# A hybrid attention and recurrence trunk: one input projection of the recurrence moved from the sliding-window branch to the first differential-attention head

## The chip, the cores and the metric

The kernel runs on one core of one Trainium2 chip. The metric is the device time of one execution in microseconds (us). Engines are called PE (TensorE), DVE (VectorE), ACT (ScalarE), POOL (GpSimd) and SP (SyncE, which here only issues DMAs); PEld is PE's loading of weights. Most executions of a kernel agree within 0.3%.

## The reference, cut to what matters

Two layers run over 128 context tokens and 1024 latent tokens of width 1024. Each layer normalises and modulates its input to `h`, projects `h` by one wide matrix, feeds three branches, gates each branch with its own SiLU path, and merges them:

```python
(q_a, k_a, v_a, g_a, x_b, g_b, q_c, k_c, v_c, g_c, merge), gate = mixer_front(x, mod, P['norm_g'], P['w_in'])
oa = attn_a_latent(q_a, k_a, v_a, ck_a, cv_a, P['sink_a'])       # windowed attention, 8 heads
xb = centred_conv(x_b, P['conv_w'], P['conv_b'])
ob, _ = rglru_bidir(xb, st, P)                                    # gated linear recurrence, 512 channels
oc = diff_attn(q_c, k_all, v_all, lam, P['subln_c'], lam_init)    # differential attention, 4 heads
return mixer_tail(x, gate, oa, g_a, ob, g_b, oc, g_c, merge, P)
```

Everything is float32. The change concerns only when `x_b` and `g_b` are computed.

## The kernel before, in words

All 1152 tokens are held as nine tiles of 128. `h` stays in SBUF for the whole layer as a high and a low part; every float32 product is made of three matmuls (high by high, high by low, low by high) in `mm3`. A weight block of 1024 x 128 columns is loaded by one DMA into `wsraw`, cast on ACT into `wsh`, and its remainder is taken on POOL in four pieces into `wsl` (`ws_load`); the three buffers come from a ring W of seven. The block then meets the nine token tiles in three chunks of 384 columns (`ws_chunk`, 8 x 3 = 24 matmuls, one PSUM buffer `ps_s` of four). The projection to queries, keys and values works the other way round, one token tile at a time (`tok_gemm`, weights `uwh`, `uwl`), also 24 matmuls of 384 columns.

`unit_phase` is the stage around the change. In its foreground run the four heads of branch C, and then the four head pairs of branch A. Each walks over five groups of token tiles, `GR` = (0), (1,2), (3,4), (5,6), (7,8): queries are transposed (`q_conv`), scores are made (`c_probs` or `a_probs`: matmuls, row maximum on DVE, exponential on ACT), and one group later the probabilities are transposed and multiplied with the values (`c_pv` or `a_pv`, called through `flush`). At the end of a head or pair `c_finish` or `a_finish` multiplies with the SiLU gate.

Beside the foreground runs the generator `background`, which yields once after each chunk of 24 matmuls. It projects the next head's queries, keys and values (nine chunks), the current head's gate (`gate_silu`, three chunks), then the remaining queries of branch A (`a_gemm2`, nine chunks), the gates of its four pairs (three each), and the recurrence's two inputs for each of four channel tiles (`lru_x(L, ct)`, three chunks of `x_b` and three of `g_b`, stored to DRAM as `xsp` and `gsp` for the tail). `step(n)` takes `n` chunks of it. The tables say how many are taken where: `BG0` in the first C head (before its context keys, then after each group), `BGQ` in the other heads, `BGA` in branch A. Foreground calls go through `fg`, which gives their instructions a priority 2000 places ahead. The Tile framework settles the order of instructions on each engine when the kernel is built, and the engine then takes its queue in that order.

Before the change the first C head has 6+2+2+1+1+0 = 12 steps, the others 12. Branch A has 3 steps, then 2 after each of twenty groups, 43 of the 45 there are; the last two follow behind the last pair. `lru_x(L, 0)` to `lru_x(L, 3)` come behind the gates of pairs 1, 2, 3 and 3. After `unit_phase` comes the tail, which computes the recurrence from the stored tiles beside the merge projections.

Of the kernel before, what the change touches and what calls it, by code (L numbers as in the profile page):

```python
# [37 lines left out]
XPOS = 1  # L38

BGQ = (2, 2, 2, 3, 2, 1)  # L40
BG0 = (6, 2, 2, 1, 1, 0)
BGA = (3, 2, 2, 2, 2, 2)

RINGS = {"S": 26, "P": 7, "T": 2, "Q": 2, "W": 7, "D": 3, "E": 2, "cx": 1, "tab": 1}

# [9 lines left out]
def hybrid_dit_kernel(ctx, tc, I, O):  # L55
# [14 lines left out]
    def al(tag, name, *shape):  # L70

        return big.tile([128] + list(shape), F32, tag=tag, name=name, bufs=RINGS[tag])
# [13 lines left out]
    def dma(out, in_):  # L86
        nc.sync.dma_start(out=out, in_=in_)
# [13 lines left out]
    def stt(out, a, s, b, op0, op1):  # L101
        V.scalar_tensor_tensor(out=out, in0=a, scalar=s, in1=b, op0=op0, op1=op1)  # L102
# [46 lines left out]
    def split(hi, lo, raw, eh="A", el="P"):  # L149

        if eh == "A":
            acopy(r(hi), raw)
        else:
            V.tensor_copy(r(hi), raw)
        if el == "P":
            psub(r(lo), raw, hi)
        else:
            tt(V, r(lo), raw, hi, ALU.subtract)

    def ws_load(wcols, kt):  # L160

        raw = al("W", "wsraw", kt, 128)
        wcols(raw)
        hi, lo = al("W", "wsh", kt, 128), al("W", "wsl", kt, 128)
        split(hi, lo, raw)
        return hi, lo

    def w_in_cols(l, c0):
        def f(lo):
            dma(lo, I["w_in"][l, :, c0:c0 + 128].rearrange("(k p) n -> p k n", p=128))  # L170
        return f
# [19 lines left out]
    def ws_chunk(L, hi, lo, c):  # L191
        p = ps("s", 384)
        for k in range(KT):
            a, b = hchunk(L, c, k)
            mm3(p, hi[:, k, :], lo[:, k, :], a, b, k == 0, k == KT - 1)
        return p
# [153 lines left out]
    def load_wu(L, groups, early=False):  # L350

        src = I["w_in"][L.l].rearrange("(k p) n -> p k n", p=128)
        raws, w = [], []

        def conv(raw):
            m = raw.shape[1]
            hi, lo = al("W", "uwh", m, 384), al("W", "uwl", m, 384)
            split(hi, lo, raw, "A", "P")
            return [(hi[:, j, :], lo[:, j, :]) for j in range(m)]
        for k0 in (0, 3, 6):  # L360
            m = min(3, KT - k0)
            raw = al("W", "wuraw", m, 384)
            for g, c0 in enumerate(groups):
                dma(raw[:, :, 128 * g:128 * g + 128], src[:, k0:k0 + m, c0:c0 + 128])
            raws.append(raw)
            if not early:
                w += conv(raws.pop())
        for raw in raws:
            w += conv(raw)
        return w  # L370
# [72 lines left out]
    def gate_silu(L, c0, put):  # L443

        gate = al("S", "gate", NTOK)

        def f(c, p):
            t = al("D", "gt", 384)
            A.activation(out=t, in_=p, func=AF.Tanh, scale=0.5)
            stt(gate[:, c * 384:(c + 1) * 384], t, 1.0, p, ALU.add, ALU.mult)  # L450
        hi, lo = ws_load(w_in_cols(L.l, c0), KT)
        put(gate)
        for c in range(3):
            f(c, ws_chunk(L, hi, lo, c))
            yield
# [5 lines left out]
    def c_groups(h):  # L461
        return [CQC + 128 * h, CKC + 128 * h, CVC + 128 * h]
# [264 lines left out]
    def unit_phase(L):  # L727

        l = L.l
        a_groups = [CQA, CKA, CVA]  # L730
        pend = None

        done = None

        def flush():
            nonlocal pend, done
            d, done = done, None
            if pend:
                pend()
                pend = None  # L740
            if d:
                d()

        def start(h):
            u = Unit()
            if h < 4:
                L.units.append(u)
                return qkv_gemm(L, u, L.wu, (0, 1), O["nck"][0, l, :, h, :, :], O["ncv"][0, l, :, h, :],
                                V if h == 0 else None)
            L.ua = u  # L750
            return qkv_gemm(L, u, L.wu, (2, 3), O["nak"][0, l], O["nav"][0, l].rearrange("t v d -> t (v d)"))

        def background():

            for h in range(4):
                L.wu = load_wu(L, c_groups(h + 1) if h < 3 else a_groups)
                yield from start(h + 1)
                yield from gate_silu(L, CGC + 128 * h, lambda gate, u=L.units[h]: setattr(u, "gate", gate))
            L.wu2 = load_wu(L, [CQA + 128, CQA + 256, CQA + 384])
            yield from a_gemm2(L)  # L760
            for g in range(4):
                yield from gate_silu(L, CGA + 128 * g, L.gates.append)
                if g:
                    yield from lru_x(L, g - 1)
            yield from lru_x(L, 3)

        def step(n):
            for _ in range(n):
                next(bg, None)

        def fg(f, *args):
            with tc.high_priority(offset=HPO):
                return f(*args)
        for _ in start(0):
            pass
        bg = background()
        step(BG0[0])
        fg(c_kconv, L, L.units[0], 0)
        for h in range(4):
            u = L.units[h]  # L780
            u.l0 = tl("l0", 9, bufs=2)
            qn = BGQ if h else BG0
            if h:
                step(qn[0])
            fg(v_conv, u, I["cache_c_v"][0, l, :, h, :])
            for g, tiles in enumerate(GR):
                n = len(tiles)
                q = fg(q_conv, u.q[:, tiles[0]:tiles[0] + n, :, :].rearrange("p t m d -> p (t m) d"), 2 * n)
                Ps = [fg(c_probs, L, u, tiles[0], q, 0)]
                fg(flush)  # L790
                if n == 2:
                    Ps.append(fg(c_probs, L, u, tiles[1], q, 1))

                def pend(u=u, tiles=tiles, Ps=Ps, h=h, g=g):
                    if g == 0:
                        u.o = al("P", "O", 1152)
                    c_pv(L, u, tiles, Ps)
                    if g == 4:
                        nonlocal done
                        done = lambda: c_finish(L, u, h)  # L800
                    if g == 1 and h:
                        c_factor(L.units[h - 1], h - 1)
                step(qn[g + 1])
            if h < 3:
                fg(c_kconv, L, L.units[h + 1], h + 1)
            else:
                fg(a_kconv, L)
        u = L.ua
        fg(v_conv, u, I["cache_a_v"][0, l].rearrange("t v d -> t (v d)"), True)
        fg(flush)  # L810
        L.mask = al("P", "mask", 9, 128)
        dma(L.mask, I["mask"].rearrange("p (a b) -> p a b", a=9))
        step(BGA[0])
        for g in range(4):
            if g == 1:
                c_factor(L.units[3], 3)
            for n, tiles in enumerate(GR):
                i, m = tiles[0], len(tiles)
                q = fg(q_conv, (u.qs[g] if g else u.q)[:, i:i + m, :, :].rearrange("p t h d -> p (t h) d"), 2 * m)
                Ps = fg(a_probs, L, g, tiles, q)  # L820
                fg(flush)

                def pend(g=g, n=n, tiles=tiles, Ps=Ps):
                    if n == 0:
                        L.Oa = al("P", "Oa", 1152)
                    a_pv(L, g, tiles, Ps, L.Oa)
                    if n == 4:
                        nonlocal done
                        done = lambda o=L.Oa: a_finish(L, g, o)
                step(BGA[n + 1])  # L830
        fg(flush)
        fg(flush)
        for _ in bg:
            pass


    def lru_x(L, ct):

        def fx(c, p):
            t = al("D", "xt", 384)  # L840
            acopy(t, p)
            dma(xsp[ct][:, 384 * c:384 * c + 384], t)
        def fg(c, p):
            d = al("D", "gxt", 2, 384)
            t, g = d[:, 0], d[:, 1]
            A.activation(out=t, in_=p, func=AF.Tanh, scale=0.5)
            stt(g, t, 1.0, p, ALU.add, ALU.mult)
            dma(gsp[ct][:, 384 * c:384 * c + 384], g)

        for f, c0 in ((fx, CXB), (fg, CGB)):  # L850
            hi, lo = ws_load(w_in_cols(L.l, c0 + 128 * ct), KT)
            for c in range(3):
                f(c, ws_chunk(L, hi, lo, c))
                yield
# [375 lines left out]
    for l in range(DEPTH):  # L1230
        L = Lay()
# [9 lines left out]
    L = Ls[0]  # L1241
# [20 lines left out]
    for n, b0 in enumerate((0, 8, 4, 12)):  # L1262
        g = mod_rows(L.D, b0, 4)
# [24 lines left out]
    for l in range(DEPTH):  # L1288
        L = Ls[l]
# [75 lines left out]
```

## Time and profile before

| | |
|---|---|
| median of 3 timed runs | 2767.63 us (2765.0 to 2769.83) |
| the profiled execution, its own time | 2773.2 us |
| its span, first to last instruction | 2771.4 us |
| mean granted clock of PE in it | 0.99 |

The rows further down come from the profiled execution. Busy times are sums over an engine's instructions. Matmuls overlap in the array, so a matmul's duration is longer than the distance to the next one. The granted clock is 1.00 at PE's upper level (2.4 GHz) and 0.5 at its lower one (1.2 GHz); a mean between the two says how much of a window ran at each. The two layers run the same code.

### The profile page before, as it was taken

To read this page: it belongs to the slowest core of one execution; us is meant where nothing else is said; L and a number is where in the kernel's file an instruction comes from. 1 tells how busy PE (TensorE), PEld (TensorE's weight loads), DVE (VectorE), ACT (ScalarE), POOL (GpSimd) and SP (SyncE) were. 2 spreads that over 40 slices of the span, in tenths; PEclk is the share of its full clock that TensorE was granted. 3 is DMA by queue.
4 is the path that set the end of the run, shared out by engine and by line. 5 is a ranking of instruction groups with operands and counts; after the bars stand their busy time and mean duration, and the time that the engine had idled before them with its cause. 6 is when DMAs were issued, how large, how long until landed. Compare 5 with 4: busy or idle time off the path is not lost. (4 is left out here: it accounts for less than half of the span.)

```text
span 2771.4 us, 42562 instructions
## 1 busy us (share of the span) xinstructions
PE 2681.6 (97%) x15581; PEld 2543.1 (92%) x15581; DVE 1722.8 (62%) x4321; ACT 1292.8 (47%) x2576; POOL 1074.5 (39%) x1368
## 2 busy tenths in 40 slices
PE   7999999989999999999999999999999999999999
PEld 3988998989999989999889999998899999899987
DVE  4797888775664557665367887887666455432242
ACT  4465555656645644122154655656566555511210
POOL 1253454452135555232405354454321465532240
PEclk9999999999999999999999999999999999999999
DMA  6011011111333235544521011111113233432242
GB/s 237 27 34 30 25 34 35 35 44 60 100 106 105 84 130 191 185 139 123 175 70 43 17 35 31 32 42 32 44 57 119 97 96 112 137 124 90 71 143 88
DMA packets 250525, 234.15 MB, mean 84 GB/s; under 512 B 40538, under 2 KB 213964, under 8 KB 250316
## 3 DMA queue, kind: packets, MB, share of 16 engines
q1 hardware_dynamic: 250316, 231.43, 26.3%
q8 instruction: 123, 2.02, 0.3%
q14 instruction: 86, 0.70, 0.1%
HBM read 178.07 MB, written 53.31 MB: 83 GB/s over the span
## 5 line engine op out<-in xcount | busy, mean ns | idle before, releaser
L181 PE MATMUL ps_s<-h,wsh 128*128 128x384 f32 x1440 | 492.7, 342 | 1.0 <-ACT wsh L90 1.0
L182 PE MATMUL ps_s<-h,wsh 128*128 128x384 f32 x1440 | 490.6, 341 | 0.0
L183 PE MATMUL ps_s<-h,wsl 128*128 128x384 f32 x1440 | 490.4, 341 | 0.0
L93 POOL TENSOR_TENSOR wsl<-wsraw,wsh 128x256 fp32r<-128x256 f32 x320 | 262.4, 851 | 307.7 <-ACT wsh L90 223.3
L181 PEld LDWEIGHTS ps_s<-h,wsh 128*128 128x128 f32 x1440 | 272.3, 189 | 2.5 <-ACT wsh L90 1.4
L182 PEld LDWEIGHTS ps_s<-h,wsh 128*128 128x128 f32 x1440 | 272.0, 189 | 0.6
L183 PEld LDWEIGHTS ps_s<-h,wsl 128*128 128x128 f32 x1440 | 271.9, 189 | 0.5
L93 POOL TENSOR_TENSOR qkraw<-qkraw,tab 128x384 f32<-128x384 f32 (+2 forms) x92 | 135.3, 1481 | 276.6 <-DVE qkraw L93 114.6
L538 DVE TENSOR_SCALAR_CACHE_REDUCE P<-ps_s 128x384 f32<-128x384 f32 (+1 forms) x400 | 203.5, 539 | 59.9 <-PE ps_s L537 58.3
L90 ACT ACTIVATE PT<-ps_t 128x512 fp32r<-128x512 f32 (+2 forms) x304 | 161.4, 546 | 143.9 <-PE ps_o L183 76.4
L181 PE MATMUL ps_s<-uwh,h 128*128 128x384 f32 x648 | 221.4, 344 | 1.9 <-ACT h L90 1.9
L182 PE MATMUL ps_s<-uwl,h 128*128 128x384 f32 x648 | 221.5, 343 | 0.8 <-POOL uwl L93 0.8
L93 DVE TENSOR_TENSOR PT<-ps_t,PT 128x512 fp32r<-128x512 f32 (+2 forms) x304 | 187.2, 625 | 53.5 <-ACT PT L90 52.5
L183 PE MATMUL ps_s<-uwh,h 128*128 128x384 f32 x648 | 219.4, 346 | 0.0
L1046 ACT ACTIVATE mg<-ps_s 128x384 f32<-128x384 f32 x144 | 69.7, 484 | 267.4 <-DVE ps_o L102 110.7
L93 POOL TENSOR_TENSOR uwl<-wuraw,uwh 128x256 fp32r<-128x256 f32 x192 | 120.9, 664 | 181.2 <-ACT uwh L90 164.1
L548 ACT ACTIVATE P<-P,csm 128x1152 f32<-128x1152 f32 (+1 forms) x144 | 165.7, 1155 | 50.9 <-DVE csm L97 50.9
L93 POOL TENSOR_TENSOR wb<-wbraw,wb 128x256 fp32r<-128x256 f32 x96 | 81.4, 868 | 268.8 <-ACT wb L90 268.6
L181 PE MATMUL ps_s<-yh,wsh 128*128 128x384 f32 x480 | 165.6, 345 | 0.6 <-DVE asm L667 0.3
L183 PE MATMUL ps_s<-yh,wsl 128*128 128x384 f32 x480 | 164.4, 343 | 0.0
L182 PE MATMUL ps_s<-yl,wsh 128*128 128x384 f32 x480 | 164.3, 342 | 0.0
L536 PE MATMUL ps_s<-ck,qhl 128*128 128x384 f32 x384 | 137.3, 366 | 7.3 <-DVE P L538 6.8
(283 smaller groups left out, 7129.5 us busy)
## 6 DMA issues: line engine op xcount, KB each, us to landing
wsraw<-in_w_in_dram SPq DMA_DIRECT2D x80, 512.0 KB
ysp<-yr SPq DMA_DIRECT2D x32, 576.0 KB
yr<-ysp SPq DMA_DIRECT2D x32, 576.0 KB
wuraw<-in_w_in_dram SPq DMA_DIRECT2D x72, 192.0 KB
ol<-osp SPq DMA_DIRECT2D x24, 576.0 KB
modw<-in_mod_w_dram SPq DMA_DIRECT2D x20, 576.0 KB
modw<-in_mod_w_dram SPq DMA_DIRECT2D x16, 512.0 KB
woraw<-in_w_out_dram SPq DMA_DIRECT2D x16, 512.0 KB
```

Of the source, the lines that this page charges most:

```text
L90: A.activation(out=out, in_=in_, func=AF.Copy, scale=scale)
L93: e.tensor_tensor(out=out, in0=a, in1=b, op=op)
L181: T.matmul(out=out, lhsT=r(lh), rhs=r(rh), start=first, stop=False)
L182: T.matmul(out=out, lhsT=r(lh), rhs=r(rl), start=False, stop=False)
L183: newest[0] = T.matmul(out=out, lhsT=r(ll), rhs=r(rh), start=False, stop=last)
L536: T.matmul(out=p, lhsT=qh, rhs=kk, start=True, stop=False)
L538: V.tensor_scalar(out=S[:, n * c:n * c + n], in0=p, scalar1=1.0, scalar2=NEG, op0=ALU.mult, op1=ALU.max, accum_out=mx[:, mp, c:c + 1])
L548: A.activation(out=Ss[mp][:, 0:n], in_=Ss[mp][:, 0:n], func=AF.Exp, scale=0.125, bias=nm[:, mp:mp + 1], accum_out=acc)
L1046: A.activation(out=m, in_=p, func=AF.Tanh, scale=0.5)
```

## The change

`lru_x(L, 0)`, six chunks, is taken out of branch A's background and put behind the gate of the first C head; the first head's table has 18 steps for it. In branch A each of pairs 1 to 3 is now followed by its own `lru_x`. There are 39 steps there in place of 45: the first pair takes 5+3+3+2+2+1 = 16, the others 2+2+1+1+1+1 = 8 each, and the first number of each table is taken ahead of the pair's first group, also between pairs.

```diff
-BG0 = (6, 2, 2, 1, 1, 0)
-BGA = (3, 2, 2, 2, 2, 2)
+BG0 = (6, 3, 3, 2, 2, 2)
+BGA = ((5, 3, 3, 2, 2, 1), (2, 2, 1, 1, 1, 1))
...
                 yield from gate_silu(L, CGC + 128 * h, lambda gate, u=L.units[h]: setattr(u, "gate", gate))
+                if h == 0:
+                    yield from lru_x(L, 0)
             L.wu2 = load_wu(L, [CQA + 128, CQA + 256, CQA + 384])
             yield from a_gemm2(L)
             for g in range(4):
                 yield from gate_silu(L, CGA + 128 * g, L.gates.append)
                 if g:
-                    yield from lru_x(L, g - 1)
-            yield from lru_x(L, 3)
+                    yield from lru_x(L, g)
...
-        step(BGA[0])
         for g in range(4):
+            step(BGA[min(g, 1)][0])
             if g == 1:
                 c_factor(L.units[3], 3)
...
-                step(BGA[n + 1])
+                step(BGA[min(g, 1)][n + 1])
```

## Rows read from the trace of the kernel before

**Rows 1.** The page: span and busy time of PE and DVE.

```profile
span 2771.4 us, 42562 instructions
PE 2681.6 (97%) x15581; PEld 2543.1 (92%) x15581; DVE 1722.8 (62%) x4321; ACT 1292.8 (47%) x2576; POOL 1074.5 (39%) x1368
```

**Rows 2.** Windows, layer 0: from:to, length, busy of five engines, clock, DMA share, GB/s.

```profile
100.00:225.00 125.00, 117.37 (x713) 112.41 (x712) 103.74 (x306) 63.83 (x139) 51.44 (x73) 0.96 0.09 25
228.80:325.00 96.20, 93.14 (x587) 90.02 (x588) 75.69 (x237) 53.21 (x109) 43.38 (x60) 0.98 0.12 32
325.00:423.50 98.50, 96.17 (x607) 90.92 (x606) 78.68 (x248) 55.44 (x115) 45.48 (x62) 1.00 0.12 31
423.50:517.00 93.50, 89.99 (x565) 84.12 (x564) 79.19 (x252) 53.67 (x111) 44.97 (x63) 1.00 0.14 39
517.00:597.00 80.00, 72.31 (x434) 65.50 (x432) 61.42 (x168) 48.92 (x114) 44.69 (x57) 1.00 0.12 35
597.00:660.00 63.00, 62.80 (x377) 61.31 (x378) 37.25 (x123) 37.76 (x92) 16.00 (x22) 0.97 0.18 54
660.00:727.00 67.00, 67.00 (x431) 65.36 (x429) 40.29 (x113) 42.58 (x103) 11.58 (x15) 1.00 0.26 86
727.00:800.00 73.00, 73.00 (x459) 71.56 (x459) 51.20 (x115) 46.34 (x105) 25.38 (x29) 1.00 0.28 91
800.00:850.00 50.00, 48.15 (x281) 47.53 (x280) 17.82 (x31) 24.21 (x40) 15.53 (x22) 1.00 0.33 109
```

**Rows 3.** Windows, layer 1, the same columns: PE, PEld, DVE, ACT, POOL.

```profile
1480.00:1590.00 110.00, 104.39 (x652) 98.03 (x651) 92.71 (x290) 63.30 (x139) 46.35 (x66) 1.00 0.08 24
1593.60:1687.70 94.10, 91.69 (x587) 88.58 (x588) 75.24 (x237) 53.04 (x109) 43.41 (x60) 1.00 0.12 33
1687.70:1786.10 98.40, 96.13 (x607) 90.82 (x606) 78.71 (x248) 55.50 (x115) 45.47 (x62) 1.00 0.12 31
1786.10:1880.00 93.90, 90.19 (x566) 84.37 (x566) 79.39 (x252) 53.78 (x112) 45.20 (x62) 1.00 0.14 38
1880.00:1960.00 80.00, 72.50 (x433) 65.68 (x432) 61.48 (x171) 48.72 (x114) 44.50 (x57) 0.99 0.12 35
1960.00:2023.50 63.50, 63.50 (x376) 62.02 (x376) 37.02 (x121) 37.71 (x92) 15.98 (x22) 0.95 0.17 54
2023.50:2091.00 67.50, 67.18 (x429) 65.42 (x428) 40.72 (x113) 42.01 (x102) 11.60 (x15) 1.00 0.24 85
2091.00:2165.00 74.00, 74.00 (x466) 72.56 (x465) 51.54 (x116) 47.01 (x107) 26.07 (x30) 1.00 0.28 90
2165.00:2215.00 50.00, 48.15 (x273) 47.53 (x272) 17.00 (x30) 23.00 (x39) 14.84 (x21) 0.97 0.33 105
```

**Rows 4.** PE's waits in 100:225: for whom, us in total, times, longest.

```profile
PE ps_s L536 <- DVE xkv L93: 2.8, 1, 2.8
...
PE ps_s L181 <- ACT wsh L90: 1.0, 1, 1.0
```

**Rows 5.** PE's waits in 517:600.

```profile
PE ps_s L661 <- DVE gate L102: 4.2, 2, 2.7
```

**Rows 6.** Timeline of PE: start, duration, instruction, idle time before it.

```profile
126.40 0.45 PE L536 MATMUL ps_s<-xkv,qhl 128*128 128x128 f32 x1 [2.79 <-DVE xkv L93]
...
127.96 0.52 PE L182 MATMUL ps_s<-uwl,h 128*128 128x384 f32 x1
```

**Rows 7.** Windows: a stretch of the tail with chunks alone.

```profile
875.00:900.00 25.00, 25.00 (x143) 25.00 (x142) 5.37 (x9) 9.51 (x16) 12.18 (x18) 1.00 0.46 151
```

**Rows 8.** Groups of PE's instructions by shape, 600:800.

```profile
L181 PE MATMUL ps_s<-h,wsh 128*128 128x384 f32 x254 | 87.2, 344 | 0.0
```

**Rows 9.** Groups of POOL's instructions by shape, 140:260, then 500:600.

```profile
L93 POOL TENSOR_TENSOR wsl<-wsraw,wsh 128x256 fp32r<-128x256 f32 x4 | 3.4, 872 | 1.6 <-ACT wsh L90 1.6
...
L93 POOL TENSOR_TENSOR wsl<-wsraw,wsh 128x256 fp32r<-128x256 f32 x16 | 11.3, 735 | 6.5 <-ACT wsh L90 6.5
```

## Prediction

> **What bounds the kernel.** I read the page's engine table first. TensorE (PE) is busy 2681.6 of 2771.4 us, 97% [rows 1], and VectorE (DVE) follows at 62%. The change adds and removes no instruction, so it can only move the 90 us in which PE is not busy, and the time in which it runs at a lower clock. Next I cut the span into stages with the view of busy time by window, to see where those 90 us lie. In layer 0 [rows 2] the stage of branch C's first head (100:225) has PE busy 117.37 of 125.00 us, so 7.6 idle, at a mean granted clock of 0.96. The three heads after it idle 3.1, 2.3 and 3.5 us. Branch A's first pair (517:597) idles 7.7 of 80.0 us; its other three pairs idle 0.2, 0.0 and 0.0. Layer 1 repeats it [rows 3]: 5.6 in the first head, 2.4, 2.3 and 3.7 in the next, 7.5 in the first pair, then 0.0, 0.3 and 0.0. So the last three pairs have more background than they need, and the first head and the first pair have waits that nothing fills. The list of PE's waits in those two stages names them [rows 4, 5]: in the head 2.8 us for VectorE's `xkv` (the context keys), in the pair 4.2 us for VectorE's `gate`.
>
> The clock has a part. After the wait of 2.79 us that ends at 126.40 the next matmuls of 384 columns last 0.52 us [rows 6], and the stage's mean clock is 0.96: PE stood still, and then ran for a while at the lower of its two levels (1.2 GHz for 2.4). Counted at full speed that is (1-0.96) x 125 = 5.0 us at most. I add this to the idle time of a stage: first head 12.6 us in layer 0 and 5.6 in layer 1; the other heads 5.0, 2.3, 3.5 (mean 3.6) and 2.4, 2.3, 3.7 (mean 2.8). For the first pair the dip falls just behind it, into 597:660 (0.97, so 1.9 us) and 1960:2023.5 (0.95, so 3.2); with its own 0.99 in layer 1 (0.8) the pair costs 7.7+1.9 = 9.6 and 7.5+0.8+3.2 = 11.5 us.
>
> **The price of a step.** A background step is one chunk of 24 matmuls of 384 columns. In a window that holds only such matmuls 143 start in 25 us [rows 7], 0.175 us each, so a step is 4.2 us of PE. `lru_x(L, 0)` has six: 25.2 us that leave the pairs and enter the first head, in each layer. Moved at equal speed that is worth nothing. Only idle time that is filled, or newly opened, counts.
>
> **First head, 12 steps to 18.** The quota between its groups goes from 2, 2, 1, 1, 0 to 3, 3, 2, 2, 2, close to the later heads' 2, 2, 3, 2, 1. What it can win is its excess over them: 12.6 - 3.6 = 9.0 us in layer 0, 5.6 - 2.8 = 2.8 in layer 1. Lower bound of the gain: 0, because the six steps are queued behind the head's own gate steps, and the wait at 126.40 comes before any of them; upper bound 11.8. I take half, 5.9, since the largest wait of layer 0 (2.8 of 7.6 us of idle time) is out of reach and the later groups are not.
>
> **First pair, 13 steps to 16.** Five steps (for 3) come ahead of its first group, then 3, 3, 2, 2, 1, and 2 more before the next pair's first group, where today none stand. The cost to win is 9.6 + 11.5 = 21.1 us over both layers. Bounds 0 and 21.1. Half again, 10.5: the wait of 2.7 us at the seam gets a chunk or two before it, but what the matmul waits for is VectorE, which is 77% busy there (61.42 of 80) and has not less to do than before.
>
> **The last three pairs, 30 steps to 24, and 2 that were left over for the end.** In 600:800 the matmuls of L181 on the weight-stationary chunks are 254 [rows 8], eight to a chunk: 32 chunks, 133 of 200 us. The pairs' own matmuls are thus 67 us, 22 a pair. With eight steps a pair is 22 + 34 = 56 us of PE for some 66 now. VectorE's work of 37.25, 40.29 and 51.20 us a pair [rows 2] stays, so its share rises from 59 and 60% in the first two to about 69% (their mean of 38.8 in 56; the third window already holds work of the tail). ScalarE's goes from 60-64% to 72% (40.2 in 56). Bounds of the new idle time: 0 as today, and 3% of the time as in a C head, where VectorE is 79 to 85% busy (3.0 of 96): 1.7 us a pair, 10 us over six. 69% lies less than half way between 60% and those, so I take 0.7 a pair, 4.2 us. **The end of the stage.** Two chunks, 8.4 us, that now run after the last group no longer do; what covers there is the tail's first merge chunk. The end window idles 1.9 us in each layer with them. Bounds 0 and 2 x 1.9; I take 1 us a layer, 2 in all.
>
> **What else moves, at nothing.** With the six steps go two weight loads, two ScalarE casts, eight GpSimd splits, six evacuations (three of them with a VectorE operation) and six stores on SP's queue, past the next head's weight loads. The DMA engines are 9% busy in the first head against 18-28% in the pairs; GpSimd 41%. The cover is ring W's seven buffers, in which the next block is split while one of three buffers is in use; where that is short today PE waits 1.0 us for a cast [rows 4], and two more loads would at that price cost 2 us a layer. Nothing waits for the stored tile before the tail.
>
> GpSimd's splits take 872 ns on average beside branch C's work and 735 ns near the first pair [rows 9], so eight of them moved cost 8 x 0.137 = 1.1 us of an engine that is idle more than half the time: nothing on the path. The Trainium skill's page "SBUF — State Buffer", section "SBUF: two separate sides", gives a rule that speaks against the move: a GpSimd instruction and a VectorE instruction with two SBUF inputs exclude each other for the whole instruction, and VectorE is the engine that head 0 waits for. The longer splits agree in direction; by that rule in full the sum below would end at the third rival's time, by the row at the forecast.
>
> **The sum.** -5.9 - 10.5 + 4.2 + 2.0 = -10.2 us. The profiled execution took 2773.2 us (span 2771.4 and 1.8 around it) and would take 2763.0. The median of the three timed runs is 2767.6, 5.6 below; on that scale the forecast is 2757.4 us.
>
> **Rivals.** (1) *The waits stay.* For it: the matmul that waits at 126.40 has chunk matmuls right behind it, by 127.96 [rows 6]; background was there and PE, which takes its queue in order, could not reach it. Work added to a queue does not help if the planner puts it behind the waiting instruction. Against: the later heads have the same instructions and lose between a third and a half as much. If it holds, the two gains are near 0, the last pairs still pay little, and the time is 2765 to 2772. Chance 0.15.
> (2) *The last pairs become bound by their own chain: slower.* Place: queries, scores, softmax and PV from one group to the next, now under ten chunks a pair without one PE wait. The gain of 16.4 us less 2 at the end is spent when each of six pairs loses 2.4 us, so when its chain needs more than 58 us. At 60 us a pair the loss is 6 x 4 = 24 and the time 2767.6 - 16.4 + 24 + 2 = 2777. For it: the first pair, with 13 steps, is 80 us long and idles 7.7. Against: that pair also carries the query projection's vector work, VectorE 77% busy. Chance 0.22, with most of its weight below 2777.
> (3) *The moved splits hold VectorE up in the first head.* Eight at 0.87 us are 7.0 us a layer, 14 in both, if VectorE stood still through each and PE with it: 2757.4 + 14 = 2771, no change. Against: GpSimd's work in a later head is as large and those heads idle less. Chance 0.05.
> (4) *Both stages fill entirely:* -11.8 - 21.1 + 4.2 + 2 = -26.7, 2741. Chance 0.10.
>
> The forecast keeps 0.48. A difference under 0.2%, 5.5 us, is about what a measurement of this kernel cannot tell from no change. Faster than that: 0.48 + 0.10 = 0.58; within: 0.15 + 0.05 = 0.20; slower: 0.22. The likeliest case by itself spans 2748 to 2762. The range for 8 in 10 leaves out the far half of (4) and the far part of (2): 2742 to 2776.
>
> **What would show it.** Right: idle time in the first head per us near 3%; the first pair some 87 us long with 4 us idle and no dip of the clock behind it; the other three pairs near 57 us each with under 1 us idle. Wrong: the same waits for `xkv` and `gate` with the same lengths (1); PE waits on `PT` or `PA` in the last three pairs, which show none today (2); splits far above 0.9 us in the first head and VectorE idle behind them (3).

## The result, and the profile after

The change makes the kernel slower: 2817.91 us against 2768.73 us in the same runs, a ratio of 1.0174 with a 95% interval of 1.0161 to 1.0186. The forecast was 2757.4 us with a range of 2742 to 2776. The profiled execution has a span of 2818.1 us, 46.7 more than before, at a mean granted clock of 0.982 against 0.99.

The page of the changed kernel has the same instruction counts of the five engines. PE is busy 18 us longer and the span is 47 us longer, so the other 28 us are idle time. Matmuls at the lower clock count as longer busy time.

```profile
span 2818.1 us, 42564 instructions
PE 2700.0 (96%) x15581; PEld 2559.3 (91%) x15581; DVE 1720.3 (61%) x4321; ACT 1293.1 (46%) x2576; POOL 1078.3 (38%) x1368
```

The windows of the changed kernel, columns as in [rows 2], say where. In layer 0 they are the first C head, the other three, the first pair, the other three with the seam behind the last, and the start of the tail.

```profile
100.00:217.00 117.00, 115.44 (x723) 114.20 (x722) 94.24 (x272) 61.59 (x124) 51.64 (x73) 1.00 0.13 40
217.00:320.00 103.00, 100.69 (x633) 95.60 (x632) 80.18 (x251) 55.89 (x116) 46.15 (x63) 1.00 0.13 35
320.00:424.00 104.00, 99.86 (x614) 94.66 (x612) 79.19 (x249) 55.46 (x115) 45.35 (x63) 0.97 0.11 29
424.00:535.00 111.00, 108.67 (x690) 103.32 (x689) 88.73 (x283) 62.71 (x135) 54.11 (x75) 1.00 0.12 33
535.00:629.50 94.50, 84.34 (x482) 77.68 (x482) 61.68 (x179) 47.70 (x110) 48.87 (x63) 0.95 0.13 37
629.50:696.00 66.50, 63.24 (x383) 61.55 (x382) 38.22 (x111) 40.25 (x99) 11.89 (x15) 0.95 0.16 51
696.00:758.00 62.00, 58.79 (x362) 56.10 (x361) 36.62 (x110) 39.79 (x98) 10.86 (x14) 0.97 0.25 84
758.00:846.00 88.00, 73.78 (x422) 68.62 (x422) 53.46 (x123) 49.46 (x112) 23.73 (x27) 0.90 0.23 74
846.00:900.00 54.00, 54.00 (x299) 54.00 (x298) 32.53 (x42) 29.93 (x40) 26.70 (x29) 0.97 0.29 96
```

Layer 1 repeats it. Shown are its first head and its four pairs.

```profile
1489.00:1605.00 116.00, 114.64 (x711) 112.22 (x710) 92.38 (x270) 58.09 (x117) 56.73 (x79) 1.00 0.15 46
...
1928.00:2025.00 97.00, 86.83 (x496) 80.21 (x495) 59.77 (x177) 47.62 (x110) 50.23 (x66) 0.96 0.14 38
2025.00:2086.00 61.00, 55.46 (x343) 52.82 (x342) 40.33 (x112) 39.91 (x98) 12.24 (x15) 0.97 0.12 41
2086.00:2151.00 65.00, 60.63 (x373) 57.61 (x372) 37.98 (x111) 39.65 (x99) 9.19 (x12) 0.97 0.25 83
2151.00:2233.00 82.00, 72.98 (x444) 68.94 (x443) 52.51 (x121) 50.50 (x113) 26.23 (x29) 0.97 0.28 91
```

I count idle time and full-speed time lost to the lower clock together, as the prediction did. The first head fell from 12.6 to 1.6 us in layer 0 and from 5.6 to 1.4 in layer 1: a gain of 15.2. The first pair rose to 10.2 + 4.7 = 14.9 and 10.2 + 3.9 = 14.1. The 9.6 and 11.5 of the prediction include the dip of the clock behind the pair; counted as here, without it, the pair lost 7.7 and 8.3 before, so the rise is 13.0. In layer 0 the three other pairs, without a single wait before, lose 3.3 + 3.3, 3.2 + 1.9 and 14.2 + 8.8 us, 34.7 together; in layer 1 7.4, 6.3 and 11.5, 25.2. The clock stands at 0.90 to 0.97 in all these windows: PE stops, and runs at its lower level for a while after.

The waits of PE in the changed kernel's pairs 1 to 3 of layer 0 (629.5:846) and in its first pair (535:629): who waited for whom, us in total, times, longest. Before the change the first list was empty; the second answers to [rows 5].

```profile
PE ps_o L710 <- ACT PT L90: 6.3, 3, 2.5
PE ps_o L710 <- DVE Oa L102: 3.1, 1, 3.1
PE ps_o L710 <- DVE PT L93: 2.6, 3, 1.2
...
```

```profile
PE ps_s L661 <- DVE gate L102: 6.3, 2, 5.6
PE ps_o L710 <- DVE PT L93: 2.2, 3, 1.1
PE ps_s L181 <- ACT qkraw L90: 1.3, 1, 1.3
...
```

The whole first list comes to 20.3 us. Of these 9.4 are waits for `PT`, the copies of the transposed probabilities; 4.4 are for `asm`, the statistics of the softmax; 5.0 are for `Oa` and 1.5 for a result's split, both behind 800 us, where the last pair ends.

The rivals were now these. **Single chunks:** the table 2, 2, 1, 1, 1, 1 leaves a two-tile group with one chunk, and nothing stands between its transposes and its PV. **Eight are too few:** the pair's chain needs more than 56 us, however its chunks are placed. **Missing work:** what counts is that six chunks have left branch A. And for the first pair: sixteen chunks are too dense beside the query projection.

### The profile page after: what moved, and what is told of

Read it like the earlier page. It is cut to its first block, busy times and chain, and to the rows that moved or that the text cites. A ratio compares the mean times of both kernels' runs of the same rounds, so it can differ in the third digit from the quotient of the medians.

```text
span 2818.1 us, 42564 instructions
## 1 busy us (share of the span) xinstructions
PE 2700.0 (96%) x15581; PEld 2559.3 (91%) x15581; DVE 1720.3 (61%) x4321; ACT 1293.1 (46%) x2576; POOL 1078.3 (38%) x1368
## 4 chain that ended last, share of the span: by engine, by line
PE 43%; DVE 5%; ACT 2%; DMA 1%; issue 1%; POOL 1%; SPq 0%; ACTq 0%; DVEq 0%; POOLq 0%
PE ps_s L181 11%; PE ps_s L182 11%; PE ps_s L183 11%; PE ps_o L182 1%; PE ps_o L181 1%; PE ps_o L183 1%; PE ps_t L565 1%; PE ps_s L536 1%; PE ps_s L537 1%; PE ps_o L710 1%; DVE P L538 1%; PE ps_t L701 1%; ACT PA L676 1%; PE ps_s L662 0%; DVE PT L93 0%
```

## The experiments

Each run is set against runs of the kernel before on the same chip; its ratio is what to compare. Diffs that begin with the old tables are against the kernel before; the loop, which in them takes each pair's first number as the change does, is left out. Diffs that begin with the change's tables are against the change, and the others against the run just above.

**The head's part alone: the move, with branch A's old table.**

```diff
-BGA = ((5, 3, 3, 2, 2, 1), (2, 2, 1, 1, 1, 1))
+BGA = ((3, 2, 2, 2, 2, 2), (0, 2, 2, 2, 2, 2))
```

> The moved first head of the change (18 steps) with branch A's old table (3, then 2 after every group), so that its 39 steps run out in the third group of the last pair. Theory 'thin table': the loss of the change sits in groups that have one chunk beside them, and in the denser first pair. Then the first pair idles some 8 us as before, pairs 1 and 2 are back at 65 to 67 us without a wait, the gain of the first head (some 18 us over both layers) stays, only the last two groups of the last pair lose (some 8 us a layer): 2760 to 2775 us. Theory 'missing work': what costs is that branch A has six chunks fewer, wherever they are missing: the last pair alone then idles 20 us a layer or more, and the time stays at 2800 to 2818.

Measured: 2785.69 us, ratio 1.0055 (1.0033 to 1.0076), between the two. Its windows for the first head and pairs 1 to 3:

```profile
100.00:215.70 115.70, 114.14 (x716) 112.91 (x715) 93.10 (x269) 60.71 (x123) 50.41 (x71) 1.00 0.14 41
608.60:674.20 65.60, 64.11 (x379) 62.51 (x380) 38.61 (x131) 38.08 (x93) 17.01 (x23) 0.95 0.17 52
674.20:741.00 66.80, 66.80 (x428) 65.17 (x427) 40.26 (x113) 42.33 (x103) 12.36 (x17) 1.00 0.24 81
741.00:826.00 85.00, 74.31 (x438) 69.75 (x437) 52.51 (x121) 49.10 (x112) 23.76 (x29) 0.93 0.27 86
```

The first head keeps its whole gain, and pairs 1 and 2 are nearly as they were (1.5 and 0.0 us idle). The last pair, whose last two groups have no chunk, loses 10.7 + 6.0 = 16.7 us, twice what I expected. Missing work is thus real, but sits where the supply ends.

**The tables of branch A alone: nothing moved.**

```diff
-BGA = (3, 2, 2, 2, 2, 2)
+BGA = ((5, 3, 3, 2, 2, 1), (2, 2, 1, 1, 1, 1))
```

> The new table of branch A (16 steps beside the first pair, 8 beside each other) on the old order of the background, nothing moved into the first head; five chunks are left over for the end. 'Thin table': the pairs stretch as in the change (first pair some 94 us, the others 62 to 67 with 5 us idle and more), without the first head's gain: 2800 to 2835 us. 'Missing work': 45 chunks are there as before, so the time is within 15 us of before, 2768 to 2783.

Measured: 2805.21 us, ratio 1.0126 (1.0098 to 1.0153). All 45 chunks are still branch A's, 40 beside the pairs and five behind them, and the kernel is 1.3% slower: the tables cost most of it. Pairs 1 and 2 take 64.7 and 64.9 us, 3.3 and 4.6 of them idle.

**Seven chunks beside a pair, before's order.**

```diff
-BGA = (3, 2, 2, 2, 2, 2)
+BGA = ((3, 2, 2, 2, 2, 2), (0, 2, 2, 1, 1, 1))
```

> The kernel before with seven chunks instead of ten beside each of branch A's last three pairs; eleven are left over for the end. It measures what a pair takes with little beside it. If a pair has a floor of its own (its chain from group to group), the pairs stay at 60 us or more and idle 8 to 12 us each, and the leftover chunks come on top: 2810 to 2850 us. If PE only packs what there is, a pair shrinks to 22 + 29 = 51 us and the time is within 10 us of before.

Measured: 2807.6 us, ratio 1.0131 (1.0104 to 1.0159). Its first two such pairs:

```profile
589.90:648.50 58.60, 53.05 (x307) 50.27 (x308) 37.40 (x127) 35.51 (x89) 14.13 (x19) 0.94 0.14 42
648.50:707.60 59.10, 55.95 (x348) 53.27 (x346) 37.79 (x110) 37.78 (x96) 8.94 (x12) 0.97 0.13 42
```

The time lies between the two that were expected. The pairs stay near 59 us, with 5.6 and 3.2 us idle. That looks like the floor of rival 2, but this table has single chunks as well; the next run separates the two.

**Eight chunks beside a pair, in twos.**

```diff
-BGA = (3, 2, 2, 2, 2, 2)
+BGA = ((3, 2, 2, 2, 2, 2), (0, 0, 2, 2, 2, 2))
```

> The kernel before with eight chunks beside each of the last three pairs, none at the pair's one-tile group and two beside each of its two-tile groups; eight chunks are left over for the end. The change has eight as well, but 2, 2, 1, 1, 1, 1. Theory 'single chunks': what loses in a pair is a two-tile group with one chunk beside its PV. Then these pairs lose no more than 2 us each and shrink to some 58 us; the time is 2768 to 2780 (only the seam and the end differ). Theory 'eight are too few': a pair loses 6 to 8 us as in the change, however the eight are placed: 2795 to 2815.

Measured: 2780.75 us, ratio 1.0045 (1.0029 to 1.0061). Its pairs 1 and 2:

```profile
588.90:641.50 52.60, 51.52 (x308) 48.79 (x309) 35.90 (x124) 32.98 (x85) 14.66 (x19) 0.94 0.15 47
641.50:705.30 63.80, 62.31 (x395) 60.05 (x394) 39.80 (x118) 42.90 (x106) 11.46 (x15) 1.00 0.16 54
```

The first windows of this run and of the one before hold 308 and 307 matmuls, seven chunks in both: with the chunks in twos they take 52.6 us and idle 1.1, with single ones 58.6 and 5.6. So the pair's chain sets no floor at 58 us. The two windows together are 116.4 us, 58 a pair, as expected. The whole run lies just above what was expected; eight chunks are left for the end.

**The whole move, in twos.** The head's part as above, and the table of the last run: 0, 0, 2, 2, 2, 2.

> The whole move into the first head (18 steps), with 13 steps beside the first pair as before and 0, 0, 2, 2, 2, 2 beside the others; 2 are left over for the end as before. 'Single chunks': the first head's gain without the pairs' loss, 2750 to 2762 us, faster than before. 'Eight are too few': the pairs lose 6 to 8 us each: 2785 to 2805 us.

Measured: 2769.68 us, ratio 1.0004 (0.9994 to 1.0013): no difference from before, and better than any run with single chunks beside the two-tile groups. It misses both expectations. The pairs idle little (2.0, 1.5 and 1.4 us in layer 0), but the stretch behind the last pair idles 3.0 of 62.0 us at a clock of 0.94.

**The dense first pair alone.**

```diff
-BGA = (3, 2, 2, 2, 2, 2)
+BGA = ((5, 3, 3, 2, 2, 1), (0, 2, 2, 2, 2, 2))
```

> The kernel before with one part of the new table alone: 5, 3, 3, 2, 2, 1 = 16 steps beside the first pair in place of 13, ten beside the others until the 45 are used up (the last pair has nine). If the denser first pair costs what the change's stage shows, the pair takes 94 us and PE loses some 16 us in it in place of 11, with one wait of 5 to 6 us for the gate's evacuation; the time is 6 to 15 us above before, 2774 to 2790. If the denser pair only suffered from its neighbours, the time is within 5 us of before.

Measured: 2776.55 us, ratio 1.0031 (1.0019 to 1.0044), 8.6 us. The wait of 5.6 us is there, within the pair. Its window, and PE's longest wait in it:

```profile
512.60:601.20 88.60, 78.47 (x444) 71.64 (x443) 60.45 (x176) 45.54 (x105) 49.03 (x64) 0.94 0.13 37
PE ps_s L661 <- DVE gate L102: 6.3, 2, 5.6
```

The timeline of this run, with PE's chunk matmuls and some lines left out, shows what it hangs on:

```profile
571.42 1.80 POOL L93 TENSOR_TENSOR qkraw<-qkraw,tab 128x768 f32<-128x768 f32 x1
...
573.30 2.08 POOL L93 TENSOR_TENSOR aq<-qkraw,qktmp 128x256 f32<-128x256 f32 x3
575.42 0.52 ACT L388 ACTIVATE qktmp<-qkraw 128x384 f32<-128x384 f32 x1 [2.53 <-POOL aq L93]
575.85 0.47 ACT L449 ACTIVATE gt<-ps_s 128x384 f32<-128x384 f32 x1
...
576.55 0.56 DVE L102 SCALAR_TENSOR_TENSOR gate<-gt,ps_s 128x384 f32<-128x384 f32 x1
...
577.17 0.80 PE L661 MATMUL ps_s<-ak,qhl 128*128 128x512 f32 x1 [5.56 <-DVE gate L102]
```

ScalarE's next square (`qktmp`) waits for GpSimd to finish the queries before it, as its buffer comes from the three of ring D (that by the code). The gate chunk's evacuation stands behind it in ScalarE's queue, so the gate's PSUM buffer isn't freed, and the score matmul that PE has next waits for that buffer.

**The same, with GpSimd's rotary products left out of those queries.** `qk_rows` skips the products with both tables, so this kernel computes the queries of pairs 1 to 3 without their rotation.

```diff
-            qk_rows(L, i0, pss, (2, 2, 2), [u.qs[g][:, i0:i0 + n, :, :] for g in (1, 2, 3)])
+            qk_rows(L, i0, pss, (2, 2, 2), [u.qs[g][:, i0:i0 + n, :, :] for g in (1, 2, 3)], rope=False)
```

> The dense first pair (16 steps) on the order of before, with the rotary products left out of the queries of pairs 1 to 3 (in the projection that runs beside the first pair: four to six of GpSimd's operations per two token tiles), so that the kernel computes those queries without their rotation. If the 5.6 us wait of PE is ScalarE held behind GpSimd's queue of that projection, with the gate's evacuations stuck behind ScalarE, then ScalarE's waits for the aq tiles go, the 5.6 us wait falls under 2 us, and the first pair is at 80 to 84 us in place of 88: 2762 to 2772. If the wait comes from something else (the gate chunks themselves, the ring of PSUM buffers), the pair stays at 87 us or more and the time at 2773 to 2780.

Measured: 2749.07 us, ratio 0.9935 (0.9915 to 0.9955). The same work of PE (445 matmuls, 444 in the run above) now takes 75.8 us:

```profile
512.70:588.50 75.80, 74.71 (x445) 69.34 (x443) 57.71 (x176) 45.36 (x106) 32.68 (x44) 1.00 0.17 46
```

GpSimd's time in the pair fell from 49.0 to 32.7 us, ScalarE's waits for `aq` are gone, and PE's waits in the pair come to 1.0 us in all. It went further than expected: the pair is 12.8 us shorter than with the products in. Part of this could be VectorE, whose busy time fell as well, but only by 2.7 us (60.45 to 57.71).

**The whole move with the dense first pair, the others in twos.** Against the change only the last three pairs' table differs, at eight steps a pair in both.

```diff
-BGA = ((5, 3, 3, 2, 2, 1), (2, 2, 1, 1, 1, 1))
+BGA = ((5, 3, 3, 2, 2, 1), (0, 0, 2, 2, 2, 2))
```

> The whole move with the change's 16 steps beside the first pair, and 0, 0, 2, 2, 2, 2 beside the others. It differs from the change in the tables of pairs 1 to 3 alone. If the parts add up, it is the run with the move in twos (2769.7) plus what the dense pair cost alone (8.4 us): 2775 to 2786, and the 32 to 42 us that then remain to the change are those of the single chunks. If the dense pair is what makes the thin pairs lose (its chunks are taken from them), it is at 2795 or more.

Measured: 2778.61 us, ratio 1.0046 (1.003 to 1.0062). Taking two chunks from in front of each pair and two from beside its one-tile group, and giving each two-tile group one more, wins 1.0174 - 1.0046 = 1.3%, 35 us. What the two chunks in front of a pair do by themselves was not measured. Its pairs 1 to 3, which idle 1.4, 1.8 and 4.8 us:

```profile
623.30:681.40 58.10, 56.75 (x360) 54.87 (x360) 39.13 (x113) 39.01 (x99) 8.86 (x11) 1.00 0.15 50
681.40:743.20 61.80, 60.01 (x375) 57.74 (x374) 39.57 (x111) 40.18 (x99) 12.17 (x16) 0.97 0.23 76
743.20:824.00 80.80, 75.98 (x472) 73.03 (x472) 53.45 (x122) 49.61 (x112) 26.13 (x29) 0.98 0.27 89
```

The timeline of PE at the same place in both, the transposes and PV of the group (1,2) of pair 1. First this run, chunk matmuls and two score matmuls left out:

```profile
641.82 1.25 PE L701 MATMUL ps_t<-ident,PA 128*128 128x128 f32 x10
...
646.91 0.28 PE L710 MATMUL ps_o<-PT,uv 128*128 128x256 f32 x1
648.25 0.76 PE L710 MATMUL ps_o<-PT,uv 128*128 128x256 f32 x5
```

Then the change:

```profile
657.62 1.25 PE L701 MATMUL ps_t<-ident,PA 128*128 128x128 f32 x10
661.01 0.38 PE L710 MATMUL ps_o<-PT,uv 128*128 128x256 f32 x1 [2.14 <-ACT PT L90]
662.51 1.22 PE L710 MATMUL ps_o<-PT,uv 128*128 128x256 f32 x4 [1.12 <-DVE PT L93]
```

Above, PE runs chunk matmuls for 3.5 us between the transposes and the PV that needs their copies from ScalarE and VectorE, and has no idle time noted. Below, nothing stands between: PE waits 2.14 and 1.12 us, and the next four PV matmuls take 1.22 us where five took 0.76: from 662 to 668 us the granted clock is 0.50. No chunk matmul starts there for 15 us.

**Half the move.** Only `x_b`'s three chunks go to the first head; `lru_x` takes two more arguments that say which of its halves it makes.

```diff
-BG0 = (6, 3, 3, 2, 2, 2)
-BGA = ((5, 3, 3, 2, 2, 1), (2, 2, 1, 1, 1, 1))
+BG0 = (6, 2, 3, 2, 1, 1)
+BGA = ((3, 2, 2, 2, 2, 2), (0, 2, 2, 2, 2, 2))
...
                 if h == 0:
-                    yield from lru_x(L, 0)
+                    yield from lru_x(L, 0, 0, 1)
...
+                if g == 1:
+                    yield from lru_x(L, 0, 1, 2)
                 if g:
                     yield from lru_x(L, g)
```

> Only the first three of the six chunks (x_b, not g_b) move into the first head, which has 6, 2, 3, 2, 1, 1 steps; branch A keeps its old table and 42 chunks. 'Thin table': about half of the first head's gain and nothing lost but the one step missing at the very end: 2755 to 2768 us. 'Missing work': three chunks fewer in branch A cost half of what six cost: 2785 to 2800.

Measured: 2764.65 us, ratio 0.9973 (0.9962 to 0.9983), faster than before. Its first head has PE busy 107.98 of 111.40 us at full clock.

**Half the move, the end's cover kept.** One chunk fewer beside each one-tile group.

```diff
-BGA = ((3, 2, 2, 2, 2, 2), (0, 2, 2, 2, 2, 2))
+BGA = ((3, 2, 2, 2, 2, 2), (0, 1, 2, 2, 2, 2))
```

> Half of the move as in the run with three chunks, with one step fewer beside each one-tile group of the last three pairs, so that two chunks are left over for the end as before. 'Missing work at the end': the 3.7 us that the last pair lost with the half move go, and it is 5 to 9 us faster than that run: 2756 to 2762 us. If the seam between pairs needs its second chunk more than the end needs cover, it is no faster than the half move: 2764 to 2772.

Measured: 2762.09 us, ratio 0.9981 (0.9972 to 0.999). Faster than before, but its ratio and that of the run above can't be told apart, so which side of the seam needs the chunk more stays open.

**The whole move with that table.**

> The whole move with 13 steps beside the first pair and 0, 1, 2, 2, 2, 2 beside the others, nine each until the 39 are used up; one is missing at the very end and none is left over. A try for the faster version. Pairs 1 and 2 lose less than in the run without a step at the one-tile group (under 4 us and 1 us), the last pair loses more (4 to 8 us a layer against 2, but the seam behind it less): 2764 to 2772. If the end decides it is slower, 2772 to 2780.

Measured: 2758.62 us, ratio 0.9970 (0.9958 to 0.9981), better than expected and faster than both kernels. The profiled execution is the fastest of its ten, 2753.49 us. Its first head and its pairs 1 to 3:

```profile
100.00:215.50 115.50, 113.94 (x715) 112.70 (x714) 92.92 (x268) 60.74 (x123) 50.15 (x71) 1.00 0.14 41
...
605.70:666.30 60.60, 59.36 (x354) 57.79 (x355) 39.23 (x129) 36.88 (x92) 17.29 (x23) 0.95 0.16 48
666.30:727.80 61.50, 61.50 (x394) 60.01 (x394) 39.05 (x112) 40.74 (x101) 12.32 (x17) 1.00 0.16 52
727.80:808.00 80.20, 77.63 (x494) 75.42 (x493) 52.53 (x124) 49.84 (x113) 24.04 (x29) 1.00 0.34 112
```

Pair 2 has nine chunks and no idle time at all. The shortage of six chunks is now spread over the one-tile groups and the end, and the last pair idles 2.6 us where the head's part alone idled 10.7.

## Why the prediction was wrong

**The last three pairs: the step that failed.** I took 0.7 us a pair, 4.2 in all, from VectorE's share: 69% lies between 60%, where pairs lose nothing, and a C head's 79 to 85%. VectorE in fact stayed at 57 to 66% in pairs 1 and 2 of both layers, since they hardly shrank, and no engine but PE was near its limit. Yet pairs 1 to 3 lost 60 us over both layers with the clock's part, against 5.6 in the windows of before [rows 2, 3], most of that left behind by the first pair's seam. A mean share of busy time does not say whether work stands in the queue at the place where PE must wait. The run that differs in these tables alone puts 35 us on it; its own pairs 1 to 3 still lose 11.5 us in layer 0. The copies `PT` are the place that the timeline shows; the other waits of the list were not taken apart.

**The first pair.** I took half of its loss back, 10.5 us, for three more steps. They cost instead: 13.0 by the profile, 8.6 us when made alone, 11.6 between the two runs of the whole move that differ in them. I had read that the matmul at the seam waits for VectorE's `gate` and named VectorE's load. Nor was the seam bare: two chunks behind the last group stood there already, and the change makes them three. In the dense runs, one step further back the gate waited for ScalarE, and ScalarE for GpSimd, which is 56% busy in that pair before [rows 2] and did not look like a limit. In the kernel before, ScalarE has no wait for `aq` in that pair. More chunks of a projection that ends on GpSimd brought its chain earlier into the queue of ScalarE, not cover for it.

**The first head.** The direction held and the size was off: 15.2 us won where I took 5.9 and allowed 11.8. I bounded it by the other heads' rate, but the head lost less than they do: with two or three steps to a group it idles 1.3%, against their 2.4 to 3.8% in layer 0. How much was won is uncertain by some us: the four runs above that keep the old first head and the products lose 14.5 to 21.4 us there over both layers, where the profile of before shows 18.2, so the gain is some 11 to 18. The wait for `xkv` is 1.6 us, but that is not the move's doing: it is 1.6 in those four runs too, so the 2.8 is not the old table's. What went are the others (`PT` 1.8, `wsh` 1.0 and `PT` 1.0 us in [rows 4]'s window, all of them still there in the four runs, none after the change), so for the first head rival 1 is out. The third C head, however, idles 3.4 to 4.1 us in both layers of every run with the whole move, against 1.8 to 2.6 with the old first head; why stays open.

**The end.** I took 1 us a layer. In the 55 us behind the last PV of branch A the change idles 1.9 and 3.0 us in the two layers, before 1.9 in both, so it cost 1.1 in all; where it hurts is inside the last pair when no chunk is left for its last groups, 16.7 us in the first experiment.

**The rivals.** Rival 2 forecast the sign, with a chance of 0.22, and its place, and the waits for `PT` that were to show it came; its time of 2777 us was far too low. Its mechanism, a chain with a floor of 58 us or more, fell: the same number of matmuls takes 52.6 us in twos and 58.6 us with single chunks. Rival 3 fell: the splits in the first head took even longer, 928 ns on average for twelve, and no wait of PE or excess of the stage came of it. The Trainium skill's page "SBUF — State Buffer", section "SBUF: two separate sides", states that a GpSimd instruction that reads SBUF and a VectorE instruction with two SBUF inputs block each other for the whole instruction. The longer splits fit it in direction. That it is the cause is not shown, as VectorE is about as busy beside the short ones (77%, 735 ns) as beside the long ones (80%, 928 ns), and its full price did not appear. Rival 4 came true for the first head, which is down to 3.0 us over both layers, and not for the first pair.

**The sum as measured.** The first head won 15 us by the profiles. The whole move in twos is level with before (+1), so some 16 us must be given back by what is left, such as the six chunks that branch A lacks, the seams and the third head; that is a difference, and its parts were not measured; the run with 0, 1, 2, 2, 2, 2 gives back only half of that and ends 0.3% faster than before. The dense first pair adds 12 and the single chunks 35: -15 + 16 + 12 + 35 = 48, against 49 measured. As each term is the difference to the next run, the sum has to close; the runs carry the 12 and the 35, not the sum.

## What to carry to other kernels

When background work is handed out between steps of a latency chain, count it at each place where the chain must wait, not per stage: the same eight chunks a pair made 1.3% of the kernel's time by their places alone. Take what must go from the steps that need no cover (here the one-tile groups) and spread it, instead of thinning every step or letting the supply run out at the end. Before putting work in front of a wait, follow the releaser back two steps: in a queue that is kept in order, an engine far from full can hold the one that must free the buffer.

## What the runs showed of the hardware that was not expected

Short stops cost more than their length. In the change's pairs 1 to 3 of layer 0 PE idles 3.3 + 3.2 + 14.2 = 20.7 us, and the mean clock of 0.95, 0.97 and 0.90 takes another 14.0 us of full-speed time.

GpSimd's split of 128x256 has no fixed duration: before, 735 ns on average from 500 to 600 us and 872 ns from 140 to 260; in the change's first head 928 ns. VectorE's share of busy time hardly tells them apart (77% in the first pair, 80% in that head).
